# Sliding windows stored slot by slot, with the last plain stores on two hardware queues

## Chip, cores, metric

One NeuronCore of one Trainium2 chip. The metric is the device time of one execution in microseconds (us). The median of several executions is given, and ratios for comparisons. ACT and DVE are the scalar and the vector engine, POOL is GpSimd, and SP is the sync engine, which here only issues transfers. The 16 DMA engines that move the data are called transfer engines. A transfer has landed when all 16 have signalled its end; landing times are read from these signals in the trace.

## The reference

The input is 16 x 64 x 64 x 64 in fp32. Every 8x8 window at stride 4 is copied out. There is no arithmetic.

```python
for i in range(15):
    for j in range(15):
        result[:, i, j] = x[:, :, 4*i:4*i + 8, 4*j:4*j + 8].copy()   # result: 16 x 15 x 15 x 64 x 8 x 8
```

16.8 MB are read and 59.0 MB are written.

## The kernel before

The input lies in SBUF as `L`. A partition is one image of the batch, one half of the channels, and one band of 16 rows (`q`, four bands). A band has four window rows, called slots. Slots 0 to 2 lie inside the band, and ACT copies them. Slot 3 crosses into the next band: DVE copies its upper half and fetches the lower half from the neighbouring partition by a shuffle. The last band has no slot 3, so of its 128 rows a slot-3 store writes only 96. The other rows carry an index out of range and are dropped.

A window (column `j`, slot `s`) of all partitions is 1.05 MB, or 0.79 MB for slot 3. It is built in a buffer `G` and stored by GpSimd (POOL) with an indirect transfer, which takes the destination of each row from a table of indices. The first twelve windows go as two halves, so that the first half can leave before the second half of the channels has arrived. The last two windows (`TAIL`) go by plain transfers of 256 KB, one per band, which SP issues on its hardware queue. Their buffers are those of the windows three places back (`BACK`).

```python
order = [(j, s) for j in range(NW) for s in range(NSLOT)]
TAIL, BACK = 2, 3
...
    g = G[u // 2][...]                       # 9 buffers of two halves
    if not last:                             # last: slot 3
        nc.scalar.copy(out=g, in_=L[:, cs, s * ST : s * ST + WS, cols])
    else:
        nc.vector.tensor_copy(out=g[:, :, 0:ST, :], in_=L[:, cs, s * ST : RB, cols])
        nc.vector.stream_shuffle(out=g[:, :, ST:WS, :], in_=L[:, cs, 0:ST, cols], mask=nxt)
    if (j, s) in order[-TAIL:]:
        g_q = g.rearrange("(m q) c r w -> q m (c r w)", q=HQ)
        for q in range(HQ - 1 if last else HQ):
            free(nc.sync.dma_start(out=o_q[q * NSLOT + s, j], in_=g_q[q]))
        return
    ...
    st = nc.gpsimd.indirect_dma_start(out=o, out_offset=..., in_=g..., ...)   # all other windows
...
for w in rest[:-TAIL]:
    window(*w, None)
at -= 2 * BACK
for w in rest[-TAIL:]:
    window(*w, None)
```

## Time and profile before

| | before |
|---|---|
| time, median of 3 | 193.47 us (193.42 to 193.57) |
| span of the profiled run | 191.4 us |
| last indirect store landed, last plain store landed | 184.48, 190.44 us |

The profiled run took 193.19 us itself.

### The profile page before, as it was taken

The numbers are of one execution on the slowest core, as the hardware profiler recorded it, in microseconds if no ns is written. First come the engines' busy times: TensorE is split into PE (matmuls) and PEld (weight loads), VectorE is DVE, ScalarE is ACT, GpSimd is POOL, SyncE is SP. The second block draws the span as 40 slices with busy tenths as digits, with TensorE's granted clock in tenths as the row PEclk, the third lists the DMA queues.
The fourth block names the chain that finished last, engine by engine and source line by source line (L and its number), as shares of the span: only waits on it lengthen the run. The fifth ranks groups of instructions, "written<-read, shape, count | busy, mean of one in ns | idle before, by whom it ended". The sixth has DMA issues, their size and how long they took to land.

```text
span 191.4 us, 479 instructions
## 1 busy us (share of the span) xinstructions
DVE 30.4 (16%) x65; ACT 86.2 (45%) x55; POOL 68.0 (36%) x75
## 2 busy tenths in 40 slices
DVE  2000050000232302301221031203030303000030
ACT  0000059400699876364566556565647473300300
POOL 0000028723367666464464343434444444400000
DMA  5999999999999999999999999999999999999785
GB/s 180 419 413 410 410 409 413 416 423 420 417 423 429 423 418 425 407 406 414 410 413 404 414 416 413 404 409 409 411 407 409 411 409 406 416 411 416 325 265 187
DMA packets 14772, 75.80 MB, mean 396 GB/s; under 512 B 2032, under 2 KB 2032, under 8 KB 9008
## 3 DMA queue, kind: packets, MB, share of 16 engines
q0 software_dynamic: 10080, 57.15, 73.3%
q1 hardware_dynamic: 2512, 10.22, 13.8%
q10 hardware_dynamic: 2176, 8.39, 11.1%
q14 instruction: 4, 0.03, 0.0%
HBM read 16.78 MB, written 62.65 MB: 415 GB/s over the span
## 4 chain that ended last, share of the span: by engine, by line
DMA 73%; issue 19%; ACT 2%; POOL 1%; DVE 1%; POOLq 0%; DVEq 0%; PEldq 0%; ACTq 0%
DMA out_dram<-G,idx 60%; DMA out_dram<-G,idx_h 13%; ACT G L111 2%; POOL out_dram L124 1%; DVE G L114 1%; DVE G L113 0%; POOLq L124 0%; POOL pi L61 0%; DVEq L113 0%; PEldq L181 0%; ACTq L111 0%
## 5 line engine op out<-in xcount | busy, mean ns | idle before, releaser
L111 ACT COPY G<-L 128x2048 f32<-128x2048 f32 (+1 forms) x54 | 84.9, 1611 | 69.1 <-DMA out_dram<-G,idx_last 25.1
L124 POOL DMA_INDIRECT out_dram<-G,idx x35 | 33.8, 966 | 45.9 <-DMA out_dram<-G,idx 41.7
L113 DVE COPY G<-L 128x1024 f32<-128x1024 f32 (+1 forms) x18 | 11.1, 614 | 152.1 <-DMA out_dram<-G,idx 76.5
L124 POOL DMA_INDIRECT out_dram<-G,idx_h x18 | 17.4, 964 | 13.9 <-DMA out_dram<-G,idx_hlast 4.8
L114 DVE STREAM_SHUFFLE G<-L 128x1024 f32<-128x1024 f32 (+1 forms) x18 | 19.6, 1091 | 0.0
L124 POOL DMA_INDIRECT out_dram<-G,idx_hlast x6 | 5.9, 989 | 27.8 <-DVE G L114 26.3
L124 POOL DMA_INDIRECT out_dram<-G,idx_last x11 | 10.6, 964 | 10.6 <-DVE G L114 5.8
L111 ACT ACT_TABLE_LOAD x1 | 1.3, 1283 | 25.9 <-DMA L<-in_x_dram 25.9
L62 DVE TENSOR_SCALAR tb<-pi 128x1 int32<-128x1 int32 x1 | 0.2, 154 | 1.0 <-POOL pi L61 1.0
L61 POOL IOTA pi<- 128x1 int32 x1 | 0.1, 119 | 0.4 <-PEq L181 0.4
L114 DVE LOAD_MASK_SELECT G<-L x18 | 0.2, 12 | 0.0
L167 POOL MEMSET const-float32-0.0<- 128x1 f32 x1 | 0.1, 98 | 0.2 <-issue 0.2
L66 DVE CUSTOM_DVE_ANT_0 tb<-tb,tc 128x2 uint16<-128x2 uint16 x1 | 0.2, 160 | 0.0
L68 DVE CUSTOM_DVE_ANT_0 idx<-tb,tc 128x2 uint16<-128x2 uint16 x1 | 0.2, 158 | 0.0
L67 DVE TENSOR_SCALAR tc<-tq 128x1 int32<-128x1 int32 x1 | 0.2, 153 | 0.0
L77 DVE TENSOR_SCALAR idx_hlast<-idx_last 128x1 int32<-128x1 int32 x1 | 0.2, 153 | 0.0
L77 DVE TENSOR_SCALAR idx_h<-idx 128x1 int32<-128x1 int32 x1 | 0.2, 154 | 0.0
L71 DVE CUSTOM_DVE_ANT_0 idx_last<-idx,tq 128x2 uint16<-128x2 uint16 x1 | 0.2, 153 | 0.0
L65 DVE TENSOR_SCALAR tb<-tb 128x1 int32<-128x1 int32 x1 | 0.2, 151 | 0.0
L70 DVE TENSOR_SCALAR tq<-tq 128x1 int32<-128x1 int32 x1 | 0.1, 147 | 0.0
L64 DVE TENSOR_SCALAR tq<-pi 128x1 int32<-128x1 int32 x1 | 0.1, 144 | 0.0
L63 DVE TENSOR_SCALAR tc<-pi 128x1 int32<-128x1 int32 x1 | 0.1, 143 | 0.0
(3 smaller groups left out, 0.3 us busy)
## 6 DMA issues: line engine op xcount, KB each, us to landing
L<-in_x_dram SPq DMA_DIRECT2D x8, 1024.0 KB, 21.1
L<-in_x_dram ACTq DMA_DIRECT2D x8, 1024.0 KB, 19.8
out_dram<-G SPq DMA_DIRECT2D x7, 256.0 KB, 4.2
out_dram<-G,idx POOLq DMA_INDIRECT x35, 18.4
out_dram<-G,idx_h POOLq DMA_INDIRECT x18, 14.1
out_dram<-G,idx_last POOLq DMA_INDIRECT x11, 18.4
out_dram<-G,idx_hlast POOLq DMA_INDIRECT x6, 11.9
```

The costliest lines, as they stand in the source:

```text
L61: nc.gpsimd.iota(pi[:, :], pattern=[[0, 1]], base=0, channel_multiplier=1)
L62: nc.vector.tensor_scalar(out=tb[:, :], in0=pi[:, :], scalar1=3, scalar2=None, op0=ALU.logical_shift_right)
L65: nc.vector.tensor_scalar(out=tb[:, :], in0=tb[:, :], scalar1=float(NWIN * CH), scalar2=None, op0=ALU.mult)
L66: nc.vector.tensor_tensor(out=tb[:, :], in0=tb[:, :], in1=tc_[:, :], op=ALU.add)
L67: nc.vector.tensor_scalar(out=tc_[:, :], in0=tq[:, :], scalar1=float(NSLOT * NW * CH), scalar2=None, op0=ALU.mult)
L68: nc.vector.tensor_tensor(out=idx[:, :], in0=tb[:, :], in1=tc_[:, :], op=ALU.add)
L71: nc.vector.tensor_tensor(out=idx_last[:, :], in0=idx[:, :], in1=tq[:, :], op=ALU.add)
L77: nc.vector.tensor_scalar(out=d[:, :], in0=e[:, :], scalar1=2.0, scalar2=None, op0=ALU.mult)
L111: nc.scalar.copy(out=g, in_=L[:, cs, s * ST : s * ST + WS, cols])
L113: nc.vector.tensor_copy(out=g[:, :, 0:ST, :], in_=L[:, cs, s * ST : RB, cols])
L114: nc.vector.stream_shuffle(out=g[:, :, ST:WS, :], in_=L[:, cs, 0:ST, cols], mask=nxt)
L124: st = nc.gpsimd.indirect_dma_start(out=o, out_offset=bass.IndirectOffsetOnAxis(ap=ix[:, 0:1], axis=0), in_=g.rearrange("p c r w -> p (c r ...
```

## The change

All columns of a slot go in turn, slot 3 first. That takes DVE's two-step windows out of the end. The plain stores at the end alternate between SP's and ACT's hardware queue.

```diff
-    order = [(j, s) for j in range(NW) for s in range(NSLOT)]
+    order = [(j, s) for s in (NSLOT - 1, *range(NSLOT - 1)) for j in range(NW)]
...
-                free(nc.sync.dma_start(out=o_q[q * NSLOT + s, j], in_=g_q[q]))
+                free((nc.sync, nc.scalar)[q % 2].dma_start(out=o_q[q * NSLOT + s, j], in_=g_q[q]))
```

## The prediction

> **What bounds the kernel now.** The kernel only copies: it reads 16.8 MB once and writes 59.0 MB (16 x 225 windows x 16 KB), so I read the transfer rows of the page first.
>
> ```profile
> span 191.4 us, 479 instructions
> ...
> GB/s 180 419 413 410 410 409 413 416 423 420 417 423 429 423 418 425 407 406 414 410 413 404 414 416 413 404 409 409 411 407 409 411 409 406 416 411 416 325 265 187
> ...
> q0 software_dynamic: 10080, 57.15, 73.3%
> q1 hardware_dynamic: 2512, 10.22, 13.8%
> q10 hardware_dynamic: 2176, 8.39, 11.1%
> ```
>
> One slice is 191.4/40 = 4.79 us. From the second slice to the 37th the transfer engines move 404 to 429 GB/s, and 75.8 MB at 412 GB/s take 184 us of the 191.4. Only the first slice and the last three are below that. Nothing a store order does can shorten the 184 us; what is in reach is the end, or a hole it makes in the middle. The chain of waits says the same: 73% of it is store transfers, while ACT has 2% and DVE 1%. So next I cut the end into stretches of 2 us (columns: stretch, length, busy time of DVE, ACT and POOL, clock, share of the 16 transfer engines, GB/s).
>
> ```profile
> 75.00:165.00 90.00, 17.88 (x30) 51.13 (x27) 38.54 (x40) 1.00 1.01 410
> 165.00:179.00 14.00, 0.00 (x0) 0.00 (x0) 0.96 (x1) 1.00 1.01 415
> 180.00:182.00 2.00, 0.27 (x1) 1.11 (x1) 0.00 (x0) 1.00 0.48 201
> 182.00:184.00 2.00, 1.62 (x3) 0.00 (x0) 0.00 (x0) 1.00 0.90 283
> 184.00:186.00 2.00, 0.00 (x0) 0.00 (x0) 0.00 (x0) 1.00 0.77 262
> 186.00:188.00 2.00, 0.00 (x0) 0.00 (x0) 0.00 (x0) 1.00 0.93 283
> 188.00:190.00 2.00, 0.00 (x0) 0.00 (x0) 0.00 (x0) 1.00 0.71 250
> ```
>
> Against 415 GB/s these five rows miss (214+132+153+132+165) x 2 us = 1.59 MB, 3.8 us of transfer time. There are two different holes. At 180 to 182 about half of the engines have nothing: the indirect stores have run out on one half of them and not on the other (the packets show eight engines done near 179.6, the other eight near 183.7). From 184 on only the plain transfers are left, and they run at 250 to 283 GB/s. Their timeline and their line:
>
> ```profile
> 179.21 1.90 ACT L111 COPY G<-L 128x2048 f32<-128x2048 f32 x1 [14.52 <-DMA out_dram<-G,idx_last]
> 181.14 6.21 SPq L118 DMA_DIRECT2D out_dram<-G  x7
> 181.73 0.69 DVE L113 COPY G<-L 128x1024 f32<-128x1024 f32 x1 [21.24 <-DMA out_dram<-G,idx]
> ...
> 182.35 1.28 DVE L114 STREAM_SHUFFLE G<-L 128x1024 f32<-128x1024 f32 x1
> ```
>
> ```profile
> L118 SPq DMA_DIRECT2D out_dram<-G x7: 536/819/1387, 181.1 to 186.2; - x7
> ...
> DMA to landing us min/median/max: 4.0/4.2/4.5
> ```
>
> Seven plain stores of 256 KB are issued one after another by SP. Each issue takes 0.54 to 1.39 us, 6.21 us in all, which is 1.835 MB/6.21 us = 296 GB/s: the issue is the pace of the end, not the transfer engines. Each lands 4.0 to 4.5 us after its issue began, so the last lands at about 186.2 + 4.2 = 190.4. The two tail windows also start late: their buffers are those of the third and second last indirect stores, so ACT waits until 179.21 and DVE until 181.73.
>
> **What the Trainium skill says.** "DMA: Bandwidth & Descriptors", section "Issuing engines are not separate DMA queues": transfers from several engines run on the same 16 engines, and a second issuer saves only sequencer time. The trace agrees on the first (one ceiling of about 420 GB/s whatever the queue); here the sequencer time is just what is short. "Perfetto Trace Analysis", section "DMA Instruction — HWDGE (DVE, Sync)": the profiled span of such an issue is lock wait and descriptor generation, not the movement, and the generator is locked for exclusive use. The first half agrees (0.6 us against 4.2 to landing). If that lock serialised two issuers, nothing would be won; at the start of this trace SP and ACT issue loads side by side, four each between 0.73 and 3.85 us, at 0.63 to 0.84 us apiece, so I expect two queues to issue nearly twice as fast. "VectorE: DVE Perf Modes", section "The perf-mode tier table": the shuffle has only the slowest mode, an fp32 copy the doubled one; the trace has 1280 against 694 ns for the same 128x1024.
>
> **The change, part by part.**
>
> *Kinds of tail.* The last two windows were (column 14, slot 2) on ACT and (14, 3) on DVE, with 4 + 3 stores. They become (13, 2) and (14, 2), both on ACT, with 4 + 4. That moves 0.26 MB from the indirect stores to the tail: 0.26/0.415 = 0.63 us earlier start, as much more at the end, no sum. The waits fall from 179.2 and 181.7 to about 178.6 and 181.1.
>
> *Issue.* Four stores go from SP and four from ACT. But ACT's order becomes copy, two issues, copy, two issues. Copy one 178.6 to 180.5; two issues at 0.6 to 1.1 us, until about 182.2 (the trace's second issue, while the indirect stores still fill half of the engines, took 1.39); copy two until 184.1, against 183.63 by DVE before. The last four issues take two turns on each queue, so the last begins near 184.8 and lands 4.2 us later: 189.0. By bytes: first packet 1.3 us after the issue (seen in the packets of before: 181.14 to 182.45), 1.05 MB at 415 GB/s is 2.5 us, and half a microsecond to the landing: 184.1 + 1.3 + 2.5 + 0.5 = 188.4. Against 190.4 this saves 1.4 to 2.0 us; with slower issues (ACT free at 183, stores at 0.8 us) 0.7.
>
> *Start.* Slot 3 first means that DVE alone makes the first 14 half windows and two whole ones, and ACT, in order of buffers, is idle until the second half of the input has landed (49.6 before). DVE makes a half in 0.96 us (copies began at 25.92, 26.88 and 27.83) and POOL issues every 1.27 us, so the first twelve are ready by 37.5, earlier than the eight stores allowed in flight let them go. Loads keep the engines full until 49 in any case. A slot-3 half store has 96 rows of 4 KB, 0.39 MB. Before, twelve first halves were 3 x 0.39 + 9 x 0.52 = 5.9 MB; now 4.7 MB. By the packets 2.4 MB of stores had gone when the loads ended; with a smaller share for stores I put 1.9 MB, so 2.8 MB, 6.7 us, are in hand at about 48. After that DVE makes two halves and then wholes of 0.79 MB in 1.95 us (403 GB/s, just under the transfer rate); the first is issued near 49.8, six microseconds before the stock ends, and from the seventh on ACT's whole windows (1.05 MB in 1.90 us) are mixed in. No hole: 0 us, at most about 2.
>
> *Middle.* Still 70 indirect stores at 0.96 us of POOL. From about 85 us all is ACT: 1.90 us for a window whose transfer takes 1.05/0.411 = 2.55 us. 0 us.
>
> Sum: -1.4 us on 193.47, so 192.0.
>
> **Rivals.** (1) DVE becomes the bound at the start. For it: 403 GB/s of supply, 8 stores in flight of only 0.39 MB. Against it: the stock of 6.7 us and the loads. It would cost 1 to 3 us: 193 to 195. (2) The tail gains nothing because ACT now copies and issues in turn, or because the issues share one generator: 193.3. For it: copy two cannot start before ACT's two issues are done, and an issue can take 1.39 us. Against it: the loads at the start. (3) The uneven halves of the transfer engines. The packets of before show the gap growing from 0.5 us at 80 to 3.9 at 170. If whole, even stores let it vanish, up to half of it, 2 us, comes on top: 190. If slot-3 stores at the start make it larger, 193 to 194. I see no reason for either: each engine gets 6 rows of 8 in a slot-3 store. (4) Neighbouring columns in turn write neighbouring 16 KB blocks instead of blocks 240 KB apart, and memory takes this better or worse. At 404 to 429 GB/s through all slots and columns nothing speaks for a limit there; 1% of rate would be 1.8 us.
>
> **Range and chances.** The tail gives 0.7 to 2.0 us; start, halves and memory may add or take about 1 us each. 190.5 to 193.5 in 8 of 10. Faster by over 2% means below 189.6: it needs the whole tail and the halves evened out, 5%. Slower by over 2%, above 197.4, needs a starved start or a lower memory rate: 3%.
>
> **What would show it.** Right: SP and ACT each with four plain stores at the end, the last begun near 185; GB/s above 330 after 184; span near 190.0; slices 6 to 14 still above 404. Wrong: slices of the start below 400 with POOL waiting for DVE's shuffle (rival 1); plain stores overlapping but each twice as long (rival 2); at 180 to 182 a share other than about 0.5 (rival 3); the middle slices moved by over 1% (rival 4).

## More of the kernel before

The lines on the transfer engines and on the end are in the prediction. For the middle, two rows of the table by stretches are wanted later (columns: stretch, length, busy time of DVE, ACT and POOL with counts, clock, share of the 16 transfer engines, GB/s):

```profile
62.00:75.00 13.00, 2.36 (x4) 10.86 (x8) 8.52 (x9) 1.00 1.02 422
75.00:100.00 25.00, 5.06 (x10) 13.19 (x7) 12.53 (x13) 1.00 1.01 410
```

## The result

The changed kernel takes 193.94 us (193.54 to 194.17, four runs), against 193.52 us (193.42 to 193.62, four runs). The ratio is 1.002, with a 95% interval of 1.0001 to 1.0038: the same within 2%, and not the gain of 0.7% that was forecast. The measured time lies above the stated range. Where two variants of different rounds are compared, the ratios count; their baselines drift by 0.2 to 0.3 us.

The page of the changed kernel, in the lines that answer to those of before:

```profile
span 192.2 us, 487 instructions
...
GB/s 180 417 413 411 409 410 411 421 420 416 415 419 420 419 422 399 393 407 399 402 412 413 407 411 413 409 409 407 413 414 411 406 416 411 406 424 421 298 273 196
...
q1 hardware_dynamic: 2368, 9.44, 12.7%
q10 hardware_dynamic: 2368, 9.44, 12.5%
```

Each hardware queue now carries half of the plain stores. The start has no hole: slices 6 to 15 stay at 410 or above. Of slices 16 to 20, all but the 18th have become slower. The same two stretches as above, then the end:

```profile
62.00:75.00 13.00, 4.84 (x15) 7.51 (x5) 9.96 (x11) 1.00 1.02 415
75.00:100.00 25.00, 0.00 (x0) 19.14 (x11) 13.36 (x15) 1.00 1.02 404
```

```profile
180.00:182.00 2.00, 0.00 (x0) 1.28 (x1) 0.00 (x0) 1.00 0.49 205
182.00:184.00 2.00, 0.00 (x0) 0.34 (x1) 0.00 (x0) 1.00 0.99 311
184.00:186.00 2.00, 0.00 (x0) 1.56 (x1) 0.00 (x0) 1.00 0.83 242
186.00:188.00 2.00, 0.00 (x0) 0.00 (x0) 0.00 (x0) 1.00 0.83 270
188.00:190.00 2.00, 0.00 (x0) 0.00 (x0) 0.00 (x0) 1.00 0.96 315
```

The hole of half the engines at 180 to 182 is there as before. From 184 on the rate averages (242+270+315)/3 = 276 GB/s, where the prediction asked for over 330; before, it was 265. Yet the transfer engines are 83 to 96% busy in these rows. The timeline of the end, and the line of the plain stores:

```profile
179.39 1.90 ACT L111 COPY G<-L 128x2048 f32<-128x2048 f32 x1 [15.67 <-DMA out_dram<-G,idx]
181.31 5.45 SPq L118 DMA_DIRECT2D out_dram<-G  x4
181.31 2.31 ACTq L118 DMA_DIRECT2D out_dram<-G  x2
183.66 1.90 ACT L111 COPY G<-L 128x2048 f32<-128x2048 f32 x1 [2.38 <-issue]
185.59 1.46 ACTq L118 DMA_DIRECT2D out_dram<-G  x2
```

```profile
L118 SPq DMA_DIRECT2D out_dram<-G x4: 537/594/1432, 181.3 to 186.2; - x4
L118 ACTq DMA_DIRECT2D out_dram<-G x4: 615/713/1662, 181.3 to 186.3; - x4
...
DMA to landing us min/median/max: 4.4/5.0/6.3
```

The second tail copy starts at 183.66, behind ACT's own issues, as the prediction feared but later than it put it. A store now takes 5.0 us from issue to landing, in place of 4.2. By the landing events of the trace the last one lands at 191.28; before it was 190.44. (The two profiled runs lie 0.83 us apart, the medians 0.42.)

### The profile page after: what moved, and what is told of

Read it like the earlier page. It is cut to its first block, busy times and chain, and to the rows that moved or that the text cites. A ratio compares the mean times of both kernels' runs of the same rounds, so it can differ in the third digit from the quotient of the medians.

```text
span 192.2 us, 487 instructions
## 1 busy us (share of the span) xinstructions
DVE 30.7 (16%) x92; ACT 86.6 (45%) x46; POOL 68.9 (36%) x75
## 4 chain that ended last, share of the span: by engine, by line
DMA 79%; issue 6%; DVE 3%; POOL 3%; ACTq 2%; ACT 2%; POOLq 0%; DVEq 0%
DMA out_dram<-G,idx 49%; DMA L<-in_x_dram 24%; DMA out_dram<-G,idx_hlast 7%; POOL out_dram L124 3%; DVE G L114 2%; ACT G L111 2%; ACTq L51 1%; ACTq L118 1%; DVE G L113 1%; POOLq L124 0%; DVEq L113 0%; ACTq L111 0%
## 5 line engine op out<-in xcount | busy, mean ns | idle before, releaser
L111 ACT COPY G<-L 128x2048 f32<-128x2048 f32 x45 | 85.3, 1898 | 49.1 <-DMA out_dram<-G,idx 41.7
L124 POOL DMA_INDIRECT out_dram<-G,idx x43 | 41.5, 964 | 53.8 <-DMA out_dram<-G,idx 48.3
L124 POOL DMA_INDIRECT out_dram<-G,idx_hlast x24 | 24.0, 1000 | 41.0 <-DVE G L114 29.7
L114 DVE STREAM_SHUFFLE G<-L 128x512 f32<-128x512 f32 (+1 forms) x27 | 20.9, 776 | 0.0
L113 DVE COPY G<-L 128x512 f32<-128x512 f32 (+1 forms) x27 | 12.9, 478 | 38.7 <-DMA L<-in_x_dram 35.0
L124 POOL DMA_INDIRECT out_dram<-G,idx_last x3 | 3.1, 1037 | 1.6 <-DVE G L114 1.3
```

The source lines that it names most:

```text
L124: st = nc.gpsimd.indirect_dma_start(out=o, out_offset=bass.IndirectOffsetOnAxis(ap=ix[:, 0:1], axis=0), in_=g.rearrange("p c r w -> p (c r ...
```

## The experiments

The theories at the outset were these. **A**: ACT's copy, issues, copy, issues in a row eat what the second queue gives. **B**: the order costs rate in the middle. **C**: a second queue gives nothing to these stores. Fourteen kernels ran; all gave right results.

**dual_only.** The old order with the second part of the change alone.

```diff
-                free(nc.sync.dma_start(...))
+                free((nc.sync, nc.scalar)[q % 2].dma_start(...))
```

> The old order, with the end's plain stores on both queues. Theory A (in the changed kernel ACT's second tail copy stands behind ACT's own two issues, and that eats what the second queue gives): here the second tail copy is DVE's, done near 183.6 as before, the last issue begins near 184.3 and lands 5 us later, 189.3 instead of 190.4, so about 1.1 us faster than before (ratio 0.994). Theory B (the order costs transfer rate in the middle, and the tail did gain): also faster, by 1 to 2 us. Theory C (a second queue gives nothing for stores): within 0.3 us of before.

192.92 us against 193.30; ratio 0.9989 (0.9972 to 1.0005), so at most a small gain, as C had it. Its stores:

```profile
L118 SPq DMA_DIRECT2D out_dram<-G x4: 599/1207/1337, 181.3 to 185.0; - x4
L118 ACTq DMA_DIRECT2D out_dram<-G x3: 613/1358/1957, 181.3 to 183.8; - x3
```

Here nothing holds ACT up, and both queues issue side by side. But the median issue has gone from 0.82 us on one queue to 1.21 and 1.36 us on two. The last store lands at 189.93, 0.5 us earlier than before; this trace is of the fastest of the six executions, 192.67 us. A and B both wanted more.

**order_only.** The new order, all plain stores on SP.

```diff
-                free((nc.sync, nc.scalar)[q % 2].dma_start(...))
+                free(nc.sync.dma_start(...))
```

> The new order, with all eight plain stores issued by SP. Theory A: eight issues at about 0.89 us from 181.3 on, the last begins near 187.5 and lands at 191.7; span about 192.5, 1 us over before (ratio 1.005 to 1.006), of which 0.5 us is the eighth plain store. Theory B: slower than before by 0.7 us or more, with the slices from 72 to 96 us at 393 to 407 GB/s as in the changed kernel. Theory C: the same time as the changed kernel.

193.81 us, ratio 1.0031 (1.001 to 1.0052), and the last landing is at 191.19: as the changed kernel with its two queues. So in the new order the second queue is worth nothing that can be seen. Slower than before by about 0.6 us (A had 1 us, B 0.7 or more), and as slow as the changed kernel, as C had it.

**dve_tail.** The changed kernel, its two tail copies moved to the idle DVE.

```diff
-        if not last:
+        if (j, s) in order[-TAIL:] and not last:
+            nc.vector.tensor_copy(out=g, in_=L[:, cs, s * ST : s * ST + WS, cols])
+        elif not last:
             nc.scalar.copy(out=g, in_=L[:, cs, s * ST : s * ST + WS, cols])
```

> The changed kernel, but its last two windows are copied by DVE, which is idle then; ACT only issues. Theory A: copy two no longer waits for ACT's issues (183.66 before, now at the landing of the second last store, about 182.0), the last issue begins near 184 instead of 186.3 and the last store lands near 189: 2 us faster than the changed kernel, 1.2 to 1.6 us faster than before. Theory C: landing moves by no more than the copy's shorter time, 0.6 us.

193.71 us, ratio 1.0033 (1.0013 to 1.0052); the changed kernel had 1.002. The expected 2 us did not come. Its timeline shows that the cause named by A was really removed:

```profile
180.66 5.61 SPq L120 DMA_DIRECT2D out_dram<-G  x4
180.66 5.77 ACTq L120 DMA_DIRECT2D out_dram<-G  x4
181.72 1.23 DVE L111 COPY G<-L 128x2048 f32<-128x2048 f32 x1 [1.09 <-DMA out_dram<-G,idx]
```

The second copy is done at 182.95 instead of 185.56, 2.6 us earlier. The issues simply became longer: four of them on each queue, at the same time, take 5.6 and 5.8 us, which is 1.4 us each. The last landing moved from 191.28 to 190.91 only. Theory A falls: ACT's row was real, but it was not what the end waited for.

**slot3_in_column.** Columns in turn as before, with slot 3 first in each, so that the tail is that of the changed kernel.

```diff
-    order = [(j, s) for s in (NSLOT - 1, *range(NSLOT - 1)) for j in range(NW)]
+    order = [(j, s) for j in range(NW) for s in (NSLOT - 1, *range(NSLOT - 1))]
```

> Columns in turn as before, but within a column slot 3 first, so that the tail is that of the changed kernel (two whole ACT windows, four stores on each queue) without slot by slot. Theory A: the tail loses as in the changed kernel, so 193.5 to 194. Theory B: the middle is that of before, slices from 72 to 96 us at 406 to 425 GB/s, the first tail copy begins near 178.6 instead of 179.4, and the time is about 0.7 us under the changed kernel's.

193.88 us, ratio 1.0032 (1.0015 to 1.005). The stretches from 62 to 75 and 75 to 100 us have their 424 and 410 GB/s back, as B expected, but the time is no better, and the first tail copy starts at 179.44. The slower middle is therefore not needed to make the loss. What this order shares with the changed kernel is the tail of eight stores; the runs so far do not show that it alone costs as much.

After these four the theory was **C2**: the plain stores themselves move more slowly than the indirect ones, whoever issues them, and an issue's duration follows that pace. Its rival **D**: the half of the engines that lags behind sets the end.

**back5.** Tail buffers that come free two windows earlier.

```diff
-    TAIL, BACK = 2, 3
+    TAIL, BACK = 2, 5
```

> The changed kernel, with the two tail windows in buffers that come free two stores earlier (5 windows back in place of 3), so that the plain stores run beside the last indirect ones. Theory A (ACT's copy, issues, copy, issues in a row on the path) has lost most of its ground: the copies by DVE moved the time by 0.2 us of the 2 expected. Theory C2 (plain stores alone keep the engines at only about 265 GB/s, from one queue or from two, because each 256 KB store costs an engine a start besides its two rows): beside the indirect stores that cost is hidden; the first tail copy near 174.3, last landing near 188.5 to 189, 2 to 2.5 us under the changed kernel. Theory D (the slower half of the engines sets the end whatever is done): also down to 188.5, with the other half idle from 184 on; D and C2 differ in the next run and in the split one.

197.73 us, ratio 1.0241 (1.0212 to 1.0269): 4 us slower, a miss of both theories. The rate near the end, by the same columns as above:

```profile
184.00:186.00 2.00, 0.00 (x0) 0.00 (x0) 0.00 (x0) 1.00 0.91 287
188.00:190.00 2.00, 0.00 (x0) 0.00 (x0) 0.00 (x0) 1.00 0.47 156
```

The plain stores now run beside the indirect ones and delay them: the last indirect store lands at 191.62 instead of about 185. The engines that were ahead finish first, and the lagging ones work alone, at half share, from 187 on. And the span goes on for 2.3 us after the last landing, which the next run explains.

**all_indirect.** The changed kernel without plain stores.

```diff
-        if (j, s) in order[-TAIL:]:
+        if False:
-    at -= 2 * BACK
```

> The changed kernel with no plain stores at the end: the last two windows go by indirect stores too, in the natural buffers. C2: the end runs at the indirect rate, 26.5 GB/s an engine; the slower half has 1.05 MB more to do after 183.7, 4.9 us, so it ends at 188.6 and lands at 189, 2 us under the changed kernel; the other half ends near 184. Theory A: the same, as ACT issues nothing. If the plain path is not what is slow, about the changed kernel's time.

194.87 us, ratio 1.0085 (1.0067 to 1.0103): slower again. But the last landing is at 189.26, within 0.3 us of what C2 said and 2.0 us before that of the changed kernel. The time is lost behind it. SP's waits near the end (waiter, waited for, us in total, times, longest) of this kernel, then of the changed one:

```profile
SPq L180 <- PEq L180: 3.0, 2, 2.5
```

```profile
SPq L181 <- PEq L181: 0.7, 2, 0.5
```

These are the closing barriers. The trace names who is late to them: GpSimd's closing DRAIN instruction starts at 169.72 and takes 22.53 us, until 192.25, which is 2.99 us after the last indirect store has landed. In back5 the same drain ends 2.90 us after the landing (194.52 and 191.62), in before 2.91 us (187.39 and 184.48), where the plain stores hide it. So an indirect store has to land 3 us ahead of the end, and the plain tail pays for itself by covering that. The same bytes through the same engines end 2 us sooner here, but not for the path alone. These stores were also queued early (last copy done at 168.6, last issue at 169.94), so the hole at 180 to 182 is gone (434 GB/s against 205). This run does not separate the two.

**dve_tail_split.** Twice as many plain stores of half the size.

```diff
-                free((nc.sync, nc.scalar)[q % 2].dma_start(out=o_q[...], in_=g_q[q]))
+                for h in range(2):
+                    free((nc.sync, nc.scalar)[q % 2].dma_start(
+                        out=o_q[...][..., h * 1024 : (h + 1) * 1024], in_=g_q[q][:, h * 1024 : (h + 1) * 1024]))
```

> DVE tail copies, and each of the eight plain stores of 256 KB cut into two of 128 KB (one row of 4 KB in place of 8 KB twice; 16 stores, same bytes). C2: a start per store, 0.15 to 0.3 us an engine, is paid eight more times: 1.2 to 2.4 us slower than the uncut one. Theory of issue (each issue takes 0.55 us or more and they are not overlapped between the two queues): slower by 4 to 5 us. If bytes alone set the pace: the same within 0.4 us.

194.36 us, ratio 1.0059 against 1.0033 uncut: about 0.5 us for eight more stores, 0.06 us each, with intervals that overlap. An issue-bound end would have cost 4 to 5 us, and this is out. The start per store that C2 put at 0.15 to 0.3 us is smaller; most of the slowness goes with the bytes.

**dual_back5.** dual_only with `BACK = 5`.

> The old order with both queues and buffers 5 windows back. C2: as in back5, 1.5 to 2.5 us under before, and 0.4 us under back5, because the old order loses nothing at 62 to 100 us. If the order mattered for the tail, back5 would be the faster one.

197.17 us, ratio 1.0188 (1.0145 to 1.0231), the same miss as back5 in the old order (by the 2% rule this one counts as unclear): the last indirect store lands at 191.31.

**twice_two_queues and twice_one_queue.** dve_tail, with the eight plain stores issued a second time, the same data to the same place. The second set runs after the last indirect store, so it is the disputed cost alone.

```diff
+    for rep in range(2):
+        for o, i, q in tail_stores:
+            free((nc.sync, nc.scalar)[q % 2].dma_start(out=o, in_=i))      # or nc.sync for all
```

> DVE tail copies, and the eight plain stores at the end are issued a second time, the same data to the same place, four on each queue. The second eight run with no indirect store left, so what they add to the time is what 2.10 MB of plain stores cost by themselves. Theory of issue (as the prediction had it): two queues issue 256 KB in 0.45 us or less, so the transfer rate of 415 GB/s decides: 5.1 us more than with one set (193.71), 198.8. C2 (the plain path itself moves 270 to 330 GB/s whoever issues): 6.4 to 7.8 us more, 200.1 to 201.5.

> The same with all sixteen on SP. Theory of issue: 0.89 us each, 7.1 us for the second eight, so 2 us over the run with two queues or more. C2: within 1 us of the run with two queues.

199.61 us with two queues (ratio 1.0342), 199.82 us with one (1.0333): no difference. The second set costs 199.61 - 193.71 = 5.9 us (the last landings, 196.80 and 190.91, say the same), so 2.10 MB at 355 GB/s. That is not the 415 of the issue theory, and better than the 330 that C2 allowed at most. One queue, then two, each with a row of the table by stretches from the time when only plain stores run:

```profile
180.56 13.68 SPq L156 DMA_DIRECT2D out_dram<-G  x16
192.00:194.00 2.00, 0.00 (x0) 0.00 (x0) 0.00 (x0) 1.00 0.94 332
```

```profile
180.59 11.74 SPq L156 DMA_DIRECT2D out_dram<-G  x8
180.59 11.91 ACTq L156 DMA_DIRECT2D out_dram<-G  x8
192.00:194.00 2.00, 0.00 (x0) 0.00 (x0) 0.00 (x0) 1.00 1.00 324
```

This is the decisive reading. Sixteen stores on one queue take 13.68 us of issue, 0.86 us each; on two queues they take 11.74 and 11.91 us side by side, 1.48 us each. The issue time per store nearly doubles when there are two issuers, and the end stays where it is. So the duration of an issue is not a cost of its own here. It is the pace at which the stores move, seen from the sequencer. The transfer engines say so too: from 188 to 195 us they are 97% busy at 341 GB/s with one queue and 95% busy at 329 GB/s with two, where the indirect stores from 165 to 179 us move 417 and 416 GB/s at 101%. The 8 KB packets of the plain stores take 384 and 382 ns on average in the two runs, those of the indirect stores 322 ns between 100 and 165 us. A generator of transfer descriptors with a fixed time per store, shared by both queues, would give the same issue times in this pair. But it would leave the engines waiting, and it does not fit dve_tail_split: eight half-size stores a queue took 8.0 us of issue there, where four whole ones took 5.8, and not twice that.

**old_tail1.** dual_only with only the last window by plain stores (`TAIL, BACK = 1, 3`).

> The old order, both queues, only the last window (three stores) by plain transfers, the one before it by an indirect store. If GpSimd's closing drain ends 3.0 us after the last indirect store has landed (22.5 us of drain in the run with indirect stores alone, ending at 192.25 against a landing at 189.26), then here: last indirect landing about 187.2, drain until 190.2, plain stores landed by about 189; span 191.1 and time 193.2, the same as before. If the drain's cost is not there, 192.0.

193.62 us, ratio 1.0015 (0.9994 to 1.0036), no better than before. GpSimd's drain ends at 190.94, 2.94 us after the last indirect landing at 188.00, and is later than the last plain landing at 189.94: here it sets the end. With two windows (dual_only) the drain ends at 188.15 and the last plain store lands at 189.93, so the balance lies between one window and two.

**slot0_first.** Still slot by slot, in the order 0, 3, 1, 2.

```diff
-    order = [(j, s) for s in (NSLOT - 1, *range(NSLOT - 1)) for j in range(NW)]
+    order = [(j, s) for s in (0, NSLOT - 1, *range(1, NSLOT - 1)) for j in range(NW)]
```

> The changed kernel with slot 0 first, then 3, 1, 2, so still slot by slot and with the same tail, but the half stores of the start are whole-slot rows by ACT and slot 3 comes as twelve or more whole windows from about 60 us on. If slot by slot as such (neighbouring columns in turn) lowers the rate from 62 to 100 us (415 and 404 GB/s, 422 and 410 before): the same here, time as the changed kernel. If it is the 24 half stores with dropped rows in the stream: 420 and 410 GB/s there, first tail copy 0.5 us earlier, time 193.4 to 193.6.

193.54 us, ratio 1.0017 (1.0001 to 1.0032). The stretch from 62 to 75 us is back at 423 GB/s and that from 75 to 100 at 407, and the first tail copy starts at 178.96, 0.43 us earlier. So it is mostly the early run of slot 3, with its 24 half stores and dropped rows, not neighbouring columns, that thins the stream. But the ratio is that of the changed kernel to within its interval.

**dual_dve and slot0_dve.** Of dual_only and slot0_first, with the whole-window tail copies on DVE, by the edit of dve_tail.

> dual_only with the copy of window (14, 2) by DVE, 1.23 us in place of 1.90 on ACT, so the first plain stores go 0.67 us earlier, while the second tail window waits for its buffer as before. If the start of the plain stores counts in full: 0.6 us under dual_only, 192.3 to 192.6 and ratio about 0.996. If the slower half of the engines sets the end: within 0.2 us of dual_only's ratio 0.999.

> slot0_first with both tail copies by DVE. If the new order's loss is made of the slot-3 halves in the stream and of ACT's copies between its issues, both are gone here: ratio 0.998 to 1.000. If it is the eighth plain store, or slot by slot as such: 1.002 as before.

dual_dve: 192.91 us against 193.18, ratio 0.9981 (0.9965 to 0.9997). The plain stores start 0.7 us earlier than in dual_only, and nearly nothing comes of it. It is the only kernel here whose interval lies below 1, so it is faster than before by 0.2%; its interval and that of dual_only overlap. slot0_dve: 193.69 us, ratio 1.0018 (1.0002 to 1.0034). ACT's row is not in it and most of the thinner stream is not (422 and 409 GB/s), and it is no faster. What it shares with all the kernels at 1.002 to 1.003 that keep two plain-stored windows and `BACK = 3` is the eighth plain store. No run went from seven plain stores to eight and changed nothing else.

## Why the prediction was wrong

- **What bounds the kernel**, and that the start holds: right. No hole appeared at the start, and DVE did not become the bound. The middle was put at 0 us and lost a little: at 62 to 100 us the rate fell by 7 and 6 GB/s, which is 13 x 7 + 25 x 6 = 241 KB, 0.6 us. That is over 1%, the sign given for rival 4 (neighbouring columns); slot0_first, which has them too, has most of it back. The first tail copy came at 179.39, not at 178.6.
- **The step that failed**, as the prediction put it: "the issue is the pace of the end, not the transfer engines". The issues do fill SP's 6.21 us, but they were long because the stores moved slowly. Doubling the issuers moved the landing by 0.5 us in the old order and by nothing in the new one. By themselves the plain stores move at 329 to 355 GB/s from one queue or two, with the transfer engines at least 95% busy. In the changed kernel's last rows they move at 242 to 315, with the engines 83 to 96% busy, so there some engine time is empty as well. Indirect stores hold 404 to 422 in the stretches shown. The term "1.05 MB at 415 GB/s is 2.5 us" was the same mistake a second time: at 355 GB/s it is 3.0 us, at the 276 of those rows 3.8. The prediction had "plain stores overlapping but each twice as long" as the sign of rival 2. In the changed kernel, where ACT's second copy stood between its issues, the medians stayed at 0.59 and 0.71 us. Where nothing stood between (dve_tail), the sign came, 1.34 and 1.48 us against 0.75 on one queue (order_only), though with another cause than a shared generator. The evidence taken against this rival, SP and ACT issuing loads side by side at 0.63 to 0.84 us, was of the first transfers of the kernel, with no others in flight.
- **ACT's row**: foreseen, mis-sized, and of no effect. Copy two began at 183.66 instead of 182.2 and ended at 185.56 instead of 184.1: copy one had begun 0.8 us late, and the two issues took 2.31 us instead of 1.7. Having the second copy done 2.6 us sooner (dve_tail) gained 0.4 us at the last landing of the trace and nothing in the ratio.
- **Landing 4.2 us after the issue**: with two queues 5.0, so the last issue at 186.32 landed at 191.28. This was no constant either but time in line: the median was 3.8 us in twice_one_queue and 6.0 in twice_two_queues.
- **"No sum" for the kinds of tail**: wrong in size. The eighth store costs an estimated 5.9/8 = 0.74 us on the plain path at the end, and the start of the tail did not come 0.6 us earlier to pay for it. In the changed kernel the middle ate it. In slot3_in_column the stores behind the one whose buffer is awaited hold 1.84 MB instead of 2.10, so that store lands as late as before although 0.26 MB less is to be stored. That would account for the 0.4 us by which the changed kernel is slower in sum, but it is argued and not isolated: slot0_dve, where the start is earlier, is not explained by it, and differences of 0.3 us are at the edge of these intervals.
- **The uneven halves** (rival 3): unchanged, as said. The share at 180 to 182 is 0.48 before and 0.49 after. The lagging half of the engines still has about 0.2 MB of indirect data when the first packets of the plain stores move, which may be why an earlier start (dual_dve, back5) helps little or hurts; no run tests this.

Left open: why the packets of these plain stores take longer at the engines. By the packet records at least half of the 8 KB packets take 309 ns, but the mean is 409 ns in before and 413 in the changed kernel. And why eight of the sixteen engines fall behind: in before the first and the last engine signal the end of a store 0.5 us apart at 80 us, and 4.2 us apart at 170.

## What to carry to other kernels

A string of long issues with no gap looks like an issue bound, but it can be back-pressure: the issuer is held up because what it issues moves slowly. Look at the transfer engines' share and rate together (0.93 for 283 GB/s at the end of before, 1.01 for 415 while the indirect stores ran), and double the stores once before paying for a second queue. Before moving a tail earlier or onto another path, ask what else it will delay, and which closing step (here GpSimd's drain, 3 us after its last store) it was hiding.

## What the Trainium skill lacked or had wrong

- "Perfetto Trace Analysis", section "DMA Instruction — HWDGE (DVE, Sync)", calls the profiled span of an issue lock wait and descriptor generation, and the same page's section "What "DMA-bound" means" takes a solid row of such slices for a bound by the sequencer. Here the span followed the movement: the same sixteen stores took 0.86 us each on one queue and 1.48 us each on two, with times 0.2 us apart and the transfer engines at least 95% busy. A solid row of issues was no proof of that bound.
- No page tells of GpSimd's closing DRAIN after indirect stores. It ends 2.9 to 3.0 us after the last of them has landed, and was 22.5 us long in all_indirect. ("VectorE: DVE Perf Modes", section "The DRAIN you can't avoid", knows a DRAIN of a kernel's end, but of some 12 ns on all engines.)
- No page has a rate for plain stores of 256 KB in 8 KB rows beside that of indirect ones: 329 to 355 GB/s against 404 to 422 on the same engines.
- No page tells of half of the sixteen engines falling behind together: 3.3 us lie between the eighth and the ninth engine's signal at the last indirect store of the kernel before.
